# Products of constants in front of TensorE's waits in a two-layer trunk of attention and experts

## The chip, the cores and the metric

The kernel runs on one core of one Trainium2 chip. The metric is the device time of one execution in microseconds (us), less is better; the median of several executions is compared.

## What is computed

A trunk of two layers on 512 tokens (one sequence, d = 1024). Layer 0 mixes with FoX attention (16 heads of 64, a forget gate per head), layer 1 with multi-head latent attention (MLA). After each mixer stands a mixture of 16 experts with gated MLPs; each token goes to 2 of them. All is float32.

```python
for i in range(DEPTH):                                   # 2 layers
    mod = silu(c) @ w_ada[i] + b_ada[i]
    sh1, sc1, g1, sh2, sc2, g2 = split(mod, 6)
    h = rmsnorm(x, mix_norm[i]) * (1 + sc1) + sh1
    y = fox_mixer(h, ...) if i % 2 == 0 else mla_mixer(h, positions, ...)
    x = x + g1 * y
    h = rmsnorm(x, ffn_norm[i]) * (1 + sc2) + sh2
    x = x + g2 * hier_moe(h, ...)

def hier_moe(h, ...):        # group top-1 of 4, expert top-2 of the 4 in that group
    combine = sum(one_hot(expert_id, 16) * w, axis=1)    # (tokens, 16), two nonzero in a row
    a, u = einsum('td,edf->tef', t, w_gate), einsum('td,edf->tef', t, w_up)     # f = 256
    return einsum('tef,efd->td', silu(a) * u * combine[..., None], w_down)
```

## The kernel before, in words

The work runs in tiles of 128 tokens, with up to 512 columns in a PSUM bank. A float32 product is made of three fp32r products of split operands (`mm3`, L128 high x high, L129 high x low weights, L130 low x high). A framework with tile pools adds the semaphores and reorders independent instructions of an engine (MLA's attention apart, which is written in a fixed order); `self.after(i)` (L1265) asks that what follows be issued behind instruction i on its engine. PSUM has banks with tags: `mm`, `s`, `pt` have two buffers each, `pv` and `ad` one (function `ps`).

The places that matter here, in the order of the program:

- **FoX stack** (`fox_stack`, L519): the normalised q and k rows (`qn`, L506) are transposed by TensorE into `ps_pt`.
- **Output projection** (`out_products`, L937 in the functions below), two halves of 512 columns by four token tiles; `moe_token` and `moe_last` then normalise each token tile, transpose it and multiply it with the router (L1051, L1076, L1079).
- **Ranks** (`dispatch`): VectorE makes the 0/1 table A of token by expert (L1119); TensorE turns it into a rank of each token within its expert by products with triangular tables (L1134, L1141). Later VectorE makes `aux`, 4 columns for each token and expert: its number and its weight in three bf16 parts (the casts L1180).
- **Slots** (`place`, `slots`, `picked`): for an expert VectorE compares the ranks with 0..99 (L1204, `oh`), TensorE picks `aux` by `oh` (four products, L1216), VectorE writes the indices `gi` (L1208), GpSimd gathers the expert's up to 100 rows `xe` from DRAM (L1269). Experts 0 to 3 are placed first, with the column of token numbers alone (`place(e, 1)`); their weights come later by L1367 (16 products of 3 columns). Experts from 4 on are placed inside the loop over experts, with all four columns, so their picks need the finished `aux`.
- **Experts** (loop of `moe`): in step e the kernel calls `place(e + 4)`, then `expert_in` (TensorE transposes `xe` into `ps_pt`, L1281; ScalarE and VectorE write `xTh`, L1283, and `xTl`, L1284), in step 0 for experts 0 and 1; then `expert_up` (24 products of 512 columns into `ps_s`) and, of the expert before, `expert_down` (`ps_mm`, L128 to L130 and L1318). Weights are loaded by SyncE's queue and split into high and low part (`weh` L136 on ScalarE, `wel` L137 on VectorE or GpSimd).
- **Result** (`result_add`): the experts' rows come back by indirect DMA (`yd` in DRAM, layer 0 into `yg`, layer 1 into `xo`), and TensorE adds them up (L1422, and L1425 for the rows of the last experts, which were kept in SBUF).

Of the kernel before, what the change touches and what calls it, by code (L numbers as in the profile page):

```python
# [19 lines left out]
P = 128  # L20
# [27 lines left out]
NFIRST = 2  # L48
HPOOL = (3,)
# [31 lines left out]
class Trunk:  # L81
# [4 lines left out]
    def setup(self):  # L86
# [28 lines left out]

        self.first32 = c.tile([P, 1], F32, name="first32")
# [7 lines left out]

    def mm3(self, out, lhs, rhs, start, stop):
        mm = self.nc.tensor.matmul
        (lh, ll), (rh, rl) = lhs, rhs
        mm(out, lh, rh, start=start, stop=False)  # L128
        mm(out, lh, rl, start=False, stop=False)  # L129
        mm(out, ll, rh, start=False, stop=stop)  # L130
# [249 lines left out]
    def pv(self, pool, V2, PT, h, hl, oT):  # L380
# [59 lines left out]
    def fox_begin(self, hT, pool):  # L440
# [7 lines left out]
        def rows(t, ks):  # L448
            for k in ks:
                self.mm3(ps[t][:, :384], [x[:, k, t * P:(t + 1) * P] for x in hT], ws[k], k == 0, k == KC - 1)  # L450
# [39 lines left out]
    def fox_proj(self, ws, hT, t):  # L490
        ts = slice(t * P, t * P + P)
        p = self.ps("mm")
        for k in range(KC):
            self.mm3(p[:, :384], [x[:, k, ts] for x in hT], ws[k], k == 0, k == KC - 1)
        return p
# [16 lines left out]
    def fox_stack(self, qn, g2, KL, slots):  # L512
# [198 lines left out]
    def mla_latents(self, x, xs, kept, begun, lat, pool, slots, fills):  # L711
# [13 lines left out]
        for t in range(NT):  # L725
# [3 lines left out]
            self.result_add(xt, two[t], t, kept, "ss")  # L729
# [205 lines left out]
    def out_products(self, p, oS, ws, t, ks):  # L935
        for k in ks:
            self.mm3(p, [x[:, t * P:(t + 1) * P] for x in oS[k]], ws[k], k == 0, k == KC - 1)  # L937
# [17 lines left out]
    def proj_out(self, pool, oS, ws, ps, wsrc, g1, x_in, after, finish):  # L955
# [7 lines left out]
        for c in range(2):  # L963
# [78 lines left out]
    def moe_token(self, x, G, SH, wr, lg, t, pool):  # L1042
# [4 lines left out]
        q = self.ps("s")[:, 0:4 + N_EXP]  # L1047
# [12 lines left out]
    def moe_last(self, x, G, SH, wr, lg, pool):  # L1060
# [8 lines left out]
        for half in range(2):  # L1069
# [4 lines left out]
            p = self.ps(("pv", "ad")[half]).rearrange("p (k t) -> p k t", k=4)  # L1074
# [3 lines left out]
            for k in range(k4):  # L1078
                nc.tensor.matmul(q, xT[:, k, :], w[:, half * k4 + k, :], start=(half == 0 and k == 0),  # L1079
                                 stop=(half == 1 and k == k4 - 1))  # L1080
# [16 lines left out]
    def dispatch(self, lg, mp, pool, tmp, lay):  # L1097
# [26 lines left out]
        diff, rest = tok(self.ps("pt")), tok(self.ps("pt"))  # L1124
# [86 lines left out]
    def picked(self, oh, aux):  # L1211
# [3 lines left out]
        for t in range(NT):  # L1215
            self.nc.tensor.matmul(q[:CAP, 0:n], oh[:, t, :], aux[:, t, :], start=(t == 0), stop=(t == NT - 1))  # L1216
# [56 lines left out]
    def expert_in(self, xe, pool):  # L1273
# [14 lines left out]
    def expert_up(self, ws, xT, w, pool):  # L1288

        nc = self.nc  # L1290
        p = self.ps("s")[:CAP]
# [8 lines left out]
    def expert_down(self, a, ws, gi, g2, pool, keep=False, rows=None):  # L1300
# [13 lines left out]
        for c in range(2):  # L1314
# [3 lines left out]
            nc.tensor.matmul(p, hT[:, 1, :], ws[1][:, cs], start=False, stop=True)  # L1318
# [15 lines left out]
    def moe(self, lay, rk, g2, loads, raws, downs, xp, kept):  # L1334
# [21 lines left out]
        for e in range(PLACE):  # L1356
            with self.after(placed[-2] if e > 1 else None):
# [19 lines left out]
        for e in range(N_EXP + 1):  # L1377
            if e < N_EXP:
# [36 lines left out]
    def result_add(self, xt, two, t, kept, tags, done=None):  # L1415
# [14 lines left out]
    def combine(self, x, out, lay, kept, ring):  # L1430
# [6 lines left out]
        for t in range(NT):  # L1437
# [4 lines left out]
            self.result_add(xs[t], two[t], t, kept, [CTAG[(2 * t + c) % 3] for c in range(2)], done)  # L1442
# [200 lines left out]
```

## Time and profile before

| | |
|---|---|
| median of three executions | 1106.43 us (1104.5, 1106.43, 1106.9) |
| the profiled execution | 1113.87 us |
| its span (first to last instruction) | 1112.1 us |
| mean granted clock of TensorE | 0.929 of full speed |
| busy: TensorE, VectorE, ScalarE, GpSimd | 87%, 74%, 54%, 32% |

The profiled execution took 7.4 us more than the median; 1.8 us of it lie outside the span. A busy TensorE may still run at the half clock, so its busy time is read together with the granted clock.

### The profile page before, as it was taken

The numbers are of one execution on the slowest core, as the hardware profiler recorded it, in microseconds if no ns is written. First come the engines' busy times: TensorE is split into PE (matmuls) and PEld (weight loads), VectorE is DVE, ScalarE is ACT, GpSimd is POOL, SyncE is SP. The second block draws the span as 40 slices with busy tenths as digits, with TensorE's granted clock in tenths as the row PEclk, the third lists the DMA queues.
The fourth block names the chain that finished last, engine by engine and source line by source line (L and its number), as shares of the span: only waits on it lengthen the run. The fifth ranks groups of instructions, "written<-read, shape, count | busy, mean of one in ns | idle before, by whom it ended". The sixth has DMA issues, their size and how long they took to land.

```text
span 1112.1 us, 16807 instructions
## 1 busy us (share of the span) xinstructions
PE 970.9 (87%) x5298; PEld 737.9 (66%) x5298; DVE 819.1 (74%) x1918; ACT 600.0 (54%) x1318; POOL 351.0 (32%) x376
## 2 busy tenths in 40 slices
PE   4788989999799858999987989989897939999996
PEld 2476868877777746666645766878686826666663
DVE  4375757777953888998866569989863778998874
ACT  5244636566742426666644446879663417566640
POOL 0011101111312655434322006555422454543332
PEclk9788989999899859999998989999898959999998
DMA  7845547577555668999969858111215787999956
GB/s 265 246 133 183 164 143 221 170 244 241 183 198 157 244 207 279 313 315 342 373 184 340 319 171 298 49 58 48 86 58 174 263 264 220 313 320 325 372 222 228
DMA packets 135732, 248.34 MB, mean 223 GB/s; under 512 B 27677, under 2 KB 56735, under 8 KB 135639
## 3 DMA queue, kind: packets, MB, share of 16 engines
q1 hardware_dynamic: 123410, 211.74, 58.0%
q0 software_dynamic: 11648, 33.39, 9.6%
q10 hardware_dynamic: 580, 2.10, 0.5%
q8 instruction: 43, 0.70, 0.3%
q14 instruction: 51, 0.41, 0.1%
HBM read 222.63 MB, written 24.55 MB: 222 GB/s over the span
## 4 chain that ended last, share of the span: by engine, by line
PE 52%; DMA 19%; DVE 12%; issue 7%; SPq 4%; ACT 3%; POOL 3%; POOLq 0%; ACTq 0%; DVEq 0%
PE ps_mm L128 6%; PE ps_mm L129 6%; PE ps_mm L130 6%; PE ps_s L398 4%; DMA wraw<-in_w_ada_dram 4%; DMA xe<-hd,gi 4%; PE ps_s L129 3%; PE ps_ad L207 3%; PE ps_s L130 3%; PE ps_s L128 3%; DMA wraw<-in_moe_w_gate_dram 3%; PE ps_pv L387 3%; PE ps_pt L364 3%; PE ps_mm L1318 2%; DMA wa<-in_w_ada_dram 2%
## 5 line engine op out<-in xcount | busy, mean ns | idle before, releaser
L136 ACT CAST weh<-wraw 128x1024 fp32r<-128x1024 f32 x128 | 133.1, 1050 | 50.7 <-PE ps_s L130 44.4
L357 POOL TENSOR_SCALAR prob<-prob,smx 128x128 f32<-128x128 f32 (+3 forms) x128 | 70.4, 551 | 283.5 <-DVE smx L356 211.8
L137 DVE TENSOR_TENSOR wel<-wraw,weh 128x1024 fp32r<-128x1024 f32 x90 | 137.9, 1557 | 19.7 <-ACT weh L136 19.3
L129 PE MATMUL ps_s<-wel,xTh 128*100 128x512 f32 x256 | 108.5, 424 | 4.5 <-DVE wel L137 3.9
L128 PE MATMUL ps_s<-weh,xTh 128*100 128x512 f32 x256 | 106.9, 419 | 3.9 <-issue 3.4
L137 POOL TENSOR_TENSOR wel<-wraw,weh 128x1024 fp32r<-128x1024 f32 x38 | 94.6, 2492 | 49.5 <-ACT weh L136 39.3
L130 PE MATMUL ps_s<-weh,xTl 128*100 128x512 f32 x256 | 107.3, 419 | 0.0
L128 PE MATMUL ps_mm<-wqh,hTh 128*128 128x384 f32 x240 | 87.2, 365 | 2.5 <-ACT hTh L317 1.9
L129 PE MATMUL ps_mm<-wql,hTh 128*128 128x384 f32 x240 | 85.3, 357 | 0.0
L130 PE MATMUL ps_mm<-wqh,hTl 128*128 128x384 f32 x240 | 84.4, 354 | 0.0
L366 ACT CAST pth<-ps_pt 128x128 fp32r<-128x128 f32 (+3 forms) x128 | 53.2, 423 | 35.7 <-PE ps_pt L364 35.4
L364 PE MATMUL ps_pt<-ident,prob 128*128 128x128 f32 x320 | 57.6, 283 | 12.8 <-POOL prob L357 7.5
L1318 PE MATMUL ps_mm<-wraw,hT 128*100 128x512 f32 x128 | 65.3, 591 | 0.0
L367 DVE TENSOR_TENSOR ptl<-ps_pt,pth 128x128 fp32r<-128x128 f32 (+3 forms) x128 | 60.5, 480 | 5.5 <-ACT pth L366 5.0
L1269 POOL DMA_INDIRECT xe<-hd,gi x32 | 47.9, 1498 | 45.7 <-PE ps_pt L1281 16.2
L128 PEld LDWEIGHTS ps_s<-weh,xTh 128*100 128x100 f32 x256 | 44.0, 173 | 22.7 <-issue 7.9
L129 PEld LDWEIGHTS ps_s<-wel,xTh 128*100 128x100 f32 x256 | 43.9, 172 | 21.0 <-DVE wel L137 5.2
L207 PE MATMUL ps_ad<-wraw,crep 128*32 128x512 f32 x320 | 44.6, 638 | 13.8 <-DMA wraw<-in_w_ada_dram 13.8
L1328 POOL DMA_DIRECT2D yd<-ye x29 | 17.6, 606 | 123.6 <-DVE ye L1319 71.5
L130 PEld LDWEIGHTS ps_s<-weh,xTl 128*100 128x100 f32 x256 | 43.6, 170 | 17.6 <-issue 3.9
L352 DVE CUSTOM_DVE_ANT_0 prob<-ps_s,negc 128x128 f32<-128x128 f32 (+1 forms) x64 | 31.0, 487 | 32.8 <-PE ps_pt L364 20.8
L364 PEld LDWEIGHTS ps_pt<-ident,prob 128*128 128x128 f32 x320 | 40.2, 145 | 21.4 <-POOL prob L357 10.0
(480 smaller groups left out, 2802.4 us busy)
## 6 DMA issues: line engine op xcount, KB each, us to landing
wraw<-in_w_ada_dram SPq DMA_DIRECT2D x84, 512.0 KB
wraw<-in_moe_w_gate_dram SPq DMA_DIRECT2D x128, 256.0 KB
wraw<-in_moe_w_up_dram SPq DMA_DIRECT2D x128, 256.0 KB
wraw<-in_moe_w_down_dram SPq DMA_DIRECT2D x64, 512.0 KB
wraw<-in_fox_w_in_dram SPq DMA_DIRECT2D x64, 192.0 KB
yd<-ye POOLq DMA_DIRECT2D x29, 400.0 KB, 6.9
wa<-in_w_ada_dram SPq DMA_DIRECT2D x12, 512.0 KB
negc<-cumd SPq DMA_DIRECT2D x16, 256.0 KB
```

What stands on the lines that cost most here:

```text
L128: mm(out, lh, rh, start=start, stop=False)
L129: mm(out, lh, rl, start=False, stop=False)
L130: mm(out, ll, rh, start=False, stop=stop)
L136: self.nc.scalar.copy(hi, src)
L137: (eng or self.nc.vector).tensor_sub(lo, src, hi.bitcast(F32))
L207: mm = nc.tensor.matmul(p[32 * g:32 * g + 32, :], self.crep[:, k, :], ws[g // 2][:, (g % 2) * 512:(g % 2) * 512 + 512], start=(k == 0), st ...
L357: nc.gpsimd.tensor_scalar(pr[:, :n], pr[:, :n], st[:, 2:3], 1.0, op0=OP.mult, op1=OP.mult)
L364: nc.tensor.transpose(p[:, j, :], pr[:, j * P:(j + 1) * P], self.ident)
L366: nc.scalar.copy(PT[0][sl], p[:, :i + 1, :])
L367: nc.vector.tensor_sub(PT[1][sl], p[:, :i + 1, :], PT[0][sl].bitcast(F32))
L1269: return self.nc.gpsimd.indirect_dma_start(out=xe, out_offset=None, in_=self.hd, in_offset=bass.IndirectOffsetOnAxis(ap=gi, axis=0), bound ...
L1318: nc.tensor.matmul(p, hT[:, 1, :], ws[1][:, cs], start=False, stop=True)
```

## The change

A helper `busy(p, n, behind)` issues n bf16 products of the constant identity with itself (128 columns, repeated four times: 512) into a PSUM tile p, whose contents the next products or transposes overwrite; nobody reads these products. They are issued behind a given instruction. A table `BUSY` gives the number for each place (a pair: layer 0 and layer 1). In all 146 products are added, each with its load of weights; no instruction of the other engines is added or removed. Some calls return their last product so that `busy` can stand behind it.

```diff
+BUSY = {"stack": 14, "out": 6, "norm": 5, "last": 3, "rank": (10, 18), "slot": (5, 9), "xe0": (4, 0), "up0": (8, 0),
+        "xe1": (0, 14), "result": (20, 16)}
...
+    def busy(self, p, n, behind=None):
+
+        with self.after(behind):
+            for _ in range(n):
+                self.nc.tensor.matmul(p.rearrange("p (k t) -> p k t", k=4), self.identb,
+                                      self.identb.unsqueeze(1).to_broadcast([P, 4, P]), start=True, stop=True)
...
             p = self.ps("pt")
+            if u == 0 and not self.stacked:
+                self.busy(p, BUSY["stack"], self.qkv)
+                self.stacked = True
...
+                if ps and t == 0:
+                    self.busy(self.ps("pt"), BUSY["out"], self.out_last if c else self.pv_last)
...
+        if t == NT - 2:
+            self.busy(q, BUSY["norm"], self.out_last)
...
+            if half == 0:
+                self.busy(p, BUSY["last"], self.out_last)
...
+        diff, rest = self.ps("pt"), self.ps("pt")
+        self.busy(diff, BUSY["rank"][lay], self.routed)
...
-            self.nc.tensor.matmul(q[:CAP, 0:n], oh[:, t, :], aux[:, t, :], start=(t == 0), stop=(t == NT - 1))
+            self.pick = self.nc.tensor.matmul(q[:CAP, 0:n], oh[:, t, :], aux[:, t, :], start=(t == 0), stop=(t == NT - 1))
...
+            if half == 0 and busy:
+                self.busy(p, busy, behind)
...
+        p = self.ps("s")
+        if busy:
+            self.busy(p, busy, self.turned)
...
+            if e == PLACE - 1:
+                self.busy(self.ps("mm"), BUSY["slot"][lay], self.pick)
...
-                        xT[a] = self.expert_in(xes[a], ep)
+                        xT[a] = self.expert_in(xes[a], ep, (BUSY["xe0"], BUSY["xe1"])[a][lay] if e == 0 else 0,
+                                               self.pick if a == 0 else self.turned)
...
-                mid[e] = self.expert_up(ws[e], xT[e], w[e], ep)
+                mid[e] = self.expert_up(ws[e], xT[e], w[e], ep, BUSY["up0"][lay] if e == 0 else 0)
...
+            if t == 0 and c == 0:
+                self.busy(p, BUSY["result"][lay], self.down_last if lay else None)
```

Line numbers of the changed kernel are higher: L128 to L130 become L139 to L141, L1216 becomes L1240, L1281 L1308, L1367 L1399; the added products are L133.

TensorE's order in layer 0, from the picks to expert 0's first products, before (L1216 x1 the last pick of expert 3, L1281 x8 the transposes of expert 0's rows, x4 half of expert 1's):

```order
L1216 LDWEIGHTS oh
L1216 MATMUL ps_pv<-aux,oh 100x1
L1281 MATMUL ps_pt<-ident,xe 128x100 x8
L128 MATMUL ps_s<-weh,xTh 100x512
L129 MATMUL ps_s<-wel,xTh 100x512
L1281 MATMUL ps_pt<-ident,xe 128x100 x4
L130 MATMUL ps_s<-weh,xTl 100x512
```

And with the change (L1399 stands 16 times; L1240 x4 columns are the picks of experts 4, 5 and 6 in turn; L133 into `ps_pt` is "xe0", into `ps_s` is "up0"; the pair of a pick and four transposes, shown once, stands twice):

```order
L1240 MATMUL ps_pv<-aux,oh 100x1
...
L1399 MATMUL ps_pv<-aux,oh 100x3
...
L1240 MATMUL ps_pv<-aux,oh 100x4
L133 LDWEIGHTS identb
L133 MATMUL ps_pt<-identb 128x512
...
L1308 MATMUL ps_pt<-ident,xe 128x100 x8
...
L1240 MATMUL ps_pv<-aux,oh 100x4
L1308 MATMUL ps_pt<-ident,xe 128x100 x4
...
L133 MATMUL ps_s<-identb 128x512
...
L139 MATMUL ps_s<-weh,xTh 100x512
```

In the call of `place(4)` just ahead, `self.pick` became the last pick of expert 4, and "xe0" is issued behind that one. So the weights' picks, the picks of experts 4 to 6 and all transposes of expert 1 now stand in front of expert 0's first product; before, the 16 picks of the weights stood behind its first 23 products and expert 4's picks later still.

In layer 1 "xe0" and "up0" are zero. There the order of before was, row for row, that of layer 0 shown first. With the change it is (L133 into `ps_pt` is "xe1", 14 times):

```order
L1240 MATMUL ps_pv<-aux,oh 100x1
L1308 MATMUL ps_pt<-ident,xe 128x100 x8
L139 MATMUL ps_s<-weh,xTh 100x512
L140 MATMUL ps_s<-wel,xTh 100x512
L133 LDWEIGHTS identb
L133 MATMUL ps_pt<-identb 128x512
...
L1308 MATMUL ps_pt<-ident,xe 128x100 x4
L141 MATMUL ps_s<-weh,xTl 100x512
```

Here only the 14 products came in, between expert 0's second product and expert 1's transposes; the picks stayed where they were.

## Rows read from the trace of the kernel before

**Rows 1.** The page of the profile, its head, the busy time of TensorE and VectorE (first row of part 1), and TensorE's granted clock in 40 equal slices of 27.8 us.

```profile
span 1112.1 us, 16807 instructions
...
PE 970.9 (87%) x5298; PEld 737.9 (66%) x5298; DVE 819.1 (74%) x1918; ACT 600.0 (54%) x1318; POOL 351.0 (32%) x376
...
PEclk9788989999899859999998989999898959999998
```

**Rows 2.** What TensorE waited for (view of waits): consumer and its line, releaser, total us, times, longest us.

```profile
PE ps_ad L207 <- DMA wraw<-in_w_ada_dram: 13.8, 5, 4.7
...
PE ps_pt L1134 <- DVE A L1119: 11.9, 2, 7.3
...
PE ps_s L1422 <- DMA yg<-yd,pos: 7.8, 1, 7.8
...
PE ps_pv L1216 <- DVE gi L1208: 6.3, 6, 3.5
...
PE ps_s L1422 <- DMA xo<-yd,pos: 5.8, 1, 5.8
PE ps_pt L519 <- DVE qn L506: 4.9, 1, 4.9
...
PE ps_mm L128 <- DVE yo L974: 3.0, 2, 1.9
```

**Rows 3.** Stretches of the span: us of the stretch; busy us and instructions of PE, PEld, DVE, ACT, POOL; granted clock of PE; DMA share; GB/s.

```profile
65.50:70.50 5.00, 0.10 (x2) 0.08 (x2) 4.83 (x15) 3.76 (x11) 0.00 (x0) 1.00 0.39 115
70.50:77.40 6.90, 6.33 (x20) 5.96 (x21) 5.28 (x22) 1.85 (x9) 0.00 (x0) 0.51 0.37 118
408.60:411.90 3.30, 3.29 (x10) 2.33 (x11) 3.10 (x17) 0.85 (x2) 0.71 (x1) 0.51 0.87 216
440.00:450.00 10.00, 10.00 (x42) 6.64 (x41) 6.09 (x9) 4.66 (x6) 2.85 (x3) 0.87 1.05 300
581.40:589.20 7.80, 0.04 (x1) 0.04 (x1) 1.38 (x3) 3.86 (x9) 2.03 (x2) 0.79 0.83 279
589.20:592.80 3.60, 3.60 (x7) 1.85 (x7) 2.83 (x6) 0.00 (x0) 1.04 (x1) 0.51 1.03 415
916.50:920.50 4.00, 3.97 (x12) 2.99 (x13) 1.42 (x5) 1.54 (x2) 0.00 (x0) 0.51 0.89 238
1084.50:1090.40 5.90, 0.07 (x1) 0.08 (x1) 3.20 (x6) 1.22 (x2) 4.48 (x5) 0.77 0.81 256
1090.40:1094.60 4.20, 4.20 (x8) 2.36 (x8) 1.41 (x3) 0.00 (x0) 3.37 (x3) 0.51 0.95 352
```

**Rows 4.** TensorE in order of time, the transposes behind the first FoX projection (start us, us, line, operation, in brackets the idle time before and what ended it).

```profile
70.45 0.61 PE L519 MATMUL ps_pt<-ident,qn 128*128 128x128 f32 x2 [4.90 <-DVE qn L506]
```

**Rows 5.** TensorE in order of time, layer 0, from the fourth expert's pick to expert 0's products.

```profile
401.11 0.42 PE L1216 MATMUL ps_pv<-aux,oh 128*100 128x1 bf16 x4 [1.76 <-DVE gi L1208]
403.68 1.58 PE L1281 MATMUL ps_pt<-ident,xe 100*128 100x100 f32 x8 [2.15 <-DMA xe<-hd,gi]
408.61 0.75 PE L128 MATMUL ps_s<-weh,xTh 128*100 128x512 f32 x1 [3.35 <-issue]
...
409.58 0.87 PE L1281 MATMUL ps_pt<-ident,xe 100*128 100x100 f32 x4
...
411.92 0.39 PE L128 MATMUL ps_s<-weh,xTh 128*100 128x512 f32 x1
412.15 0.39 PE L129 MATMUL ps_s<-wel,xTh 128*100 128x512 f32 x1
...
416.30 0.87 PE L1367 MATMUL ps_pv<-aux,oh 128*100 128x3 bf16 x16
...
421.23 0.31 PE L1216 MATMUL ps_pv<-aux,oh 128*100 128x4 bf16 x4
422.51 0.47 PE L129 MATMUL ps_s<-wel,xTh 128*100 128x512 f32 x1 [0.98 <-DVE wel L137]
```

**Rows 6.** VectorE in order of time in the same stretch: two compares of ranks, one instruction of the overflow count, and the first of the casts that write aux (the last one ends at 412.39).

```profile
399.94 1.05 DVE L1204 TENSOR_TENSOR oh<-slot,rk 128x400 bf16<-128x400 bf16 x2
...
401.33 5.35 DVE L1187 TENSOR_SCALAR nt<-ce 128x16 f32<-128x16 f32 x1
...
410.73 0.23 DVE L1180 CAST aux<-we 128x64 bf16<-128x64 f32 x1
```

**Rows 7.** GpSimd in order of time in the same stretch.

```profile
401.99 4.65 POOL L137 TENSOR_TENSOR wel<-wraw,weh 128x1024 fp32r<-128x1024 f32 x2
```

**Rows 8.** TensorE in order of time, layer 0, at the end of expert 1's up products.

```profile
438.14 1.25 PE L1281 MATMUL ps_pt<-ident,xe 100*128 100x100 f32 x8 [1.33 <-DMA xe<-hd,gi]
```

**Rows 9.** TensorE in order of time, layer 1, expert 0's first products and the transposes of expert 1's tokens.

```profile
910.16 0.63 PE L129 MATMUL ps_s<-wel,xTh 128*100 128x512 f32 x1
916.53 0.92 PE L1281 MATMUL ps_pt<-ident,xe 100*128 100x100 f32 x4 [5.74 <-DMA xe<-hd,gi]
...
917.67 0.63 PE L128 MATMUL ps_s<-weh,xTh 128*100 128x512 f32 x1
918.10 0.63 PE L129 MATMUL ps_s<-wel,xTh 128*100 128x512 f32 x1
```

**Rows 10.** TensorE in order of time, layer 1, the last expert product and the first product of the result.

```profile
1083.47 1.02 PE L1318 MATMUL ps_mm<-wraw,hT 128*100 128x512 f32 x2
1090.33 2.07 PE L1422 MATMUL ps_s<-xo,ident 128*128 128x512 f32 x2 [5.83 <-DMA xo<-yd,pos]
```

More of the change, by code (lines that the diff above doesn't have):

```diff
@@ L114, in setup @@
                        allow_small_or_imprecise_dtypes=True)
+        self.stacked = False
         self.first32 = c.tile([P, 1], F32, name="first32")
@@ L129, in mm3 @@
         mm(out, lh, rl, start=False, stop=False)
-        mm(out, ll, rh, start=False, stop=stop)
+        return mm(out, ll, rh, start=False, stop=stop)
     def split(self, shape, src, name, eng=None, pool=None):
@@ L449, in rows @@
             for k in ks:
-                self.mm3(ps[t][:, :384], [x[:, k, t * P:(t + 1) * P] for x in hT], ws[k], k == 0, k == KC - 1)
+                self.qkv = self.mm3(ps[t][:, :384], [x[:, k, t * P:(t + 1) * P] for x in hT], ws[k], k == 0, k == KC - 1)
         def gates(ks):
@@ L493, in fox_proj @@
         for k in range(KC):
-            self.mm3(p[:, :384], [x[:, k, ts] for x in hT], ws[k], k == 0, k == KC - 1)
+            self.qkv = self.mm3(p[:, :384], [x[:, k, ts] for x in hT], ws[k], k == 0, k == KC - 1)
         return p
@@ L728, in mla_latents @@
                 self.advance(fills)
-            self.result_add(xt, two[t], t, kept, "ss")
+            self.result_add(0, xt, two[t], t, kept, "ss")
             nc.scalar.dma_start(x[t * P:(t + 1) * P, :], xt)
@@ L936, in out_products @@
         for k in ks:
-            self.mm3(p, [x[:, t * P:(t + 1) * P] for x in oS[k]], ws[k], k == 0, k == KC - 1)
+            self.out_last = self.mm3(p, [x[:, t * P:(t + 1) * P] for x in oS[k]], ws[k], k == 0, k == KC - 1)
     def out_begin(self, oT, wsrc, slots, out):
@@ L1073, in moe_last @@
                 pool.tile([P, k4, P], F32, name="xTl", tag="hj")
-            p = self.ps(("pv", "ad")[half]).rearrange("p (k t) -> p k t", k=4)
+            p = self.ps(("pv", "ad")[half])
+            if half == 0:
+                self.busy(p, BUSY["last"], self.out_last)
+            p = p.rearrange("p (k t) -> p k t", k=4)
             for k in range(k4):
@@ L1078, in moe_last @@
             for k in range(k4):
-                nc.tensor.matmul(q, xT[:, k, :], w[:, half * k4 + k, :], start=(half == 0 and k == 0),
-                                 stop=(half == 1 and k == k4 - 1))
+                self.routed = nc.tensor.matmul(q, xT[:, k, :], w[:, half * k4 + k, :], start=(half == 0 and k == 0),
+                                               stop=(half == 1 and k == k4 - 1))
             nc.scalar.activation(self.ps("pv" if half else "ad"), x[:, cs], AF.Square, accum_out=ssq[:, half:half + 1])
@@ L1271, in gather, with expert_in @@
             bounds_check=S - 1, oob_is_err=True)
-    def expert_in(self, xe, pool):
+    def expert_in(self, xe, pool, busy=0, behind=None):
         nc = self.nc
@@ L1286, in expert_in, with expert_up @@
         return xT
-    def expert_up(self, ws, xT, w, pool):
+    def expert_up(self, ws, xT, w, pool, busy=0):
         nc = self.nc
-        p = self.ps("s")[:CAP]
+        p = self.ps("s")
+        if busy:
+            self.busy(p, busy, self.turned)
+        p = p[:CAP]
         for k in range(KC):
@@ L1413, in collect, with result_add @@
         return out
-    def result_add(self, xt, two, t, kept, tags, done=None):
+    def result_add(self, lay, xt, two, t, kept, tags, done=None):
         nc = self.nc
@@ L1440, in done @@
                 self.nc.sync.dma_start(out[t * P:(t + 1) * P, cs], xs[t][:, cs])
-            self.result_add(xs[t], two[t], t, kept, [CTAG[(2 * t + c) % 3] for c in range(2)], done)
+            self.result_add(lay, xs[t], two[t], t, kept, [CTAG[(2 * t + c) % 3] for c in range(2)], done)
     def overflow(self, layer, rk1, end, base, novf, g2, xp, mp, raw, sp):
```

14 lines of the change are left out of this document (8 added, 6 removed).

## The prediction

> **What bounds the kernel now.** I read the page first: TensorE is busy 970.9 of 1112.1 us, and the row of its granted clock has slices at 8 tenths and below [rows 1]. So two things can be had on TensorE: its waits, and the time after a wait in which it runs at the half level. The view of waits says which waits are long [rows 2]: 11.9 us for the table A in two waits (the longer 7.3, so the shorter 4.6), 7.8 and 5.8 for the gathered results, 4.9 for `qn`, 3.5 for `gi`. The stretches behind them were read last [rows 3]: in 70.5 to 77.4, 408.6 to 411.9, 589.2 to 592.8, 916.5 to 920.5 and 1090.4 to 1094.6 the granted clock is 0.51, and TensorE is busy nearly throughout. [...] The added products are to keep it up; they shorten no wait. What they can give back is about half of the busy time in those stretches, and what they can cost is delay of what stands behind them on TensorE.
>
> **The price of a product.** A bf16 product of 512 columns is not in the trace. The nearest rows are fp32r products of 512 columns: from 411.92 to 412.15, 0.23 us at the full clock [rows 5], and from 917.67 to 918.10, 0.43 us at half [rows 9]. I take these; below them is no reason to go, since the columns are the same. [...]
>
> **Stack, 14.** 14 x 0.23 = 3.2 us stand in the wait of 4.90 ahead of L519 [rows 4] and end before `qn` comes; 1.7 us of the wait are left. In the stretch behind, 6.33 us of work run at 0.51 [rows 3], worth up to 3.1 us. Does a wait of 1.7 us keep the clock? Rows speak both ways: after the wait of 0.98 us at 422.51 the products run at full pace [rows 5], after that of 1.33 us at 438.14 the clock of 440 to 450 is 0.87 [rows 3, 8]. I take somewhat under half: -1.2, ends 0 and -3.1.
>
> **Result, 20 and 16.** In layer 0, 20 x 0.23 = 4.6 us of the wait of 7.8 [rows 2] are filled, 3.2 us stay empty; the 3.60 us behind it [rows 3] hold at most 1.8. With so much left I take -0.3. In layer 1, TensorE ends L1318 at 1084.5 and starts L1422 at 1090.33 after 5.83 us [rows 10]; 16 x 0.23 = 3.7 are filled, 2.1 stay. Behind it 4.20 us run at 0.51 [rows 3], worth 2.1, and nothing but the result and its store comes after, so whatever is saved counts in full. Half: -1.1, ends 0 and -2.1.
>
> **xe1, 14, layer 1.** They run between expert 0's second product and the transposes at 916.53, which wait 5.74 us for the gather [rows 9]. The clock there is already 0.51, so 14 x 0.43 = 6.0 us, 0.3 more than the wait, unless the clock rises within them. Behind, 3.97 us at 0.51 [rows 3] give 2.0 back. Net -1.6; at the other end 0, if the next split weights or the next gather set the pace there.
>
> **Rank and slot.** Layer 0: 10 x 0.43 = 4.3 in a wait of 4.6. Layer 1: 18 products, 4.1 to 7.7 us in a wait of 7.3; slot 9, 2.1 to 3.9 us in a wait of 3.5 [rows 2]. They can overrun by 0.4 each if the clock stays low, and speed up the small products behind if it rises: together -0.2, ends -0.8 and +0.8. Slot 5 in layer 0 delays a pick whose expert (3) is needed much later; nothing.
>
> **Out, norm, last.** In layer 1, six products at half clock are 2.6 us where the wait for `yo` is 1.9 [rows 2], so they overrun by 0.7; but the projection is a chain through VectorE's `yo` and the x tiles, not TensorE alone. Norm and last put 8 products, 1.8 us, in front of the last two router tiles of each layer, where VectorE's normalisation comes later still and hides most. Together +0.4, ends 0 and +2.5.
>
> **xe0 and up0, layer 0: the term that decides.** Not the 12 products but the place counts. "xe0" is issued behind expert 4's pick, and expert 4's pick needs `aux`. So expert 0's transposes, at 403.68 before [rows 5], wait for the end of the routing on VectorE. That end was 412.39: a stall of 5.35 us at 401.33 [rows 6], lying with GpSimd's split of weights (4.65 us at 401.99 [rows 7]), then the routing, with the first cast of `aux` at 410.73. Without the three subtractions of `xTl` that lay between the casts (they need the transposes, so now come later) `aux` is ready near 411.
>
> From there, in a row on TensorE: three compares of about 0.53 (1.05 for two [rows 6]) with the 16 picks of the weights beside them, to 412.6; expert 4's pick 0.42, to 413.0; "xe0" 4 x 0.43 = 1.7, to 414.7; eight transposes 1.58, to 416.3; twice a pick and four transposes, 2 x (0.42 + 0.87) = 2.6, to 418.9; "up0", 8 x 0.23 = 1.8, to 420.7, if the clock is up by then (8 x 0.43 = 3.4 otherwise, 422.3). Expert 0's first product starts near 420.6 instead of 408.61: **12.0 us late**.
>
> What comes back by 450: TensorE's waits of 0.98 and 1.33 us [rows 5, 8] and some 0.6 of smaller ones, 2.9, because the split weights and gathered rows are then long there; the six products that ran at half clock from 408.6 to 411.9, 6 x 0.20 = 1.2; the half clock near 440 (0.87 of 10 us means 2.6 us at half, 1.3 back, with the tail before 440 taken as 1.8); and the work that now lies ahead, 0.87 (L1367), 0.31 (pick of expert 4), eight transposes and two picks, about 2.3 in pitch. Together 8.2. From 440 on TensorE is busy 10.00 of 10 us [rows 3], with experts following one another without a wait, so what is not back by then is kept: 12.0 - 8.2 = **+3.8**, ends +1.5 (aux earlier by what VectorE is spared, full clock in up0) and +8.5 (only the moved work and the 1.2 come back).
>
> **Reordering elsewhere.** The framework orders some of VectorE's, ScalarE's and SyncE's instructions differently in the FoX stretch. No row has a price for that; the waits for `w_ada` there, 13.8 us with one of 4.7 [rows 2], show what a load that moves can matter. Zero, ends -2.5 and +2.5.
>
> **Sum.** -1.2 - 0.3 - 1.1 - 1.6 - 0.2 + 0.4 + 3.8 = -0.2 us. The profiled execution of 1113.87 us (span 1112.1, 1.8 outside it) is 7.4 above the median 1106.43; the sum is a difference and is put on the median: 1106.2 us. A measurement of this kernel tells about 0.2%, 2.2 us, from no change.
>
> **Rivals.**
>
> *The clock holds through the shortened waits.* The remains of 1.7 and 2.1 us would be like the 0.98 us at 422.51, not like 438.14. Then the whole price comes back: 3.1 + 2.1 + 2.0 + 1.8 = 9.0 instead of 4.2, so -0.2 - 4.8 = -5.0, about 1101.4. For it: in 65.5 to 70.5 the clock is still 1.00 over a wait of 4.9 us and in 581.4 to 589.2 it is 0.79 in the mean [rows 3], so it doesn't fall at once. [...] Against: 438.14.
>
> *The layer-0 delay is absorbed.* If the loads of weights bound the experts (DMA share 1.05 in 440 to 450 [rows 3]) and not TensorE, a late start would cost little: 0 instead of +3.8 gives -4.0, 1102.4. Against it, TensorE has no wait in that stretch.
>
> *The layer-0 delay is not made up (slower).* VectorE runs the picks' reads, compares and `xTl` before the split weights; if these then come late, the waits near 422 and 438 stay and the half clock with them. It takes only the splits to be as late as the start. +8.5 instead of +3.8: +4.5, 1110.9. It decides once more than 2.4 us beyond my sum are lost there.
>
> *The products do nothing for the clock (slower).* The clock falls in each remaining wait, as after 438.14, and only the delay is left: +3.8 + 0.4 = +4.2, 1110.6.
>
> **Chances.** My sum 0.40, the clock holds 0.17, absorbed 0.15, not made up 0.18, nothing for the clock 0.10. My sum is likely within 0.2%, with 0.03 of it on each side. Faster 0.35, same 0.34, slower 0.31. The range goes from 1100 (both faster rivals partly) to 1111.5 (the slower ones and a little of the reordering); my own case alone is 1104 to 1108.5.
>
> **What would show it.** In layer 0, expert 0's first product near 12 us later against the fourth pick, TensorE without waits from there to 450, and expert 1's end 2 to 6 us later than before against the start of the dispatch. In layer 1, products behind 916 at pitch 0.23, not 0.43. At the end, granted clock of the first 4 us of the result: 0.5 or 1.0. Behind the FoX wait the same. I am wrong if the picks of experts 4 to 6 don't hold up expert 0, if the FoX stretch moves by more than 2.5 us, or if a product costs clearly more than 0.23 at full clock.

## The result and the profile after

The changed kernel took 1095.97 us in the median of six executions, beside 1106.47 of the kernel before: ratio 0.9888, interval 0.986 to 0.9915. Forecast was 1106.2 with a range from 1100. So the change gained 10.5 us by the medians and about 12 by the ratio, where the sum said none.

The page after (span, busy time of TensorE, its granted clock in 40 slices), to be read against [rows 1]:

```profile
span 1092.4 us, 17112 instructions
...
PE 989.2 (91%) x5444; PEld 738.3 (68%) x5444; DVE 816.8 (75%) x1918; ACT 598.8 (55%) x1318; POOL 349.3 (32%) x376
...
PEclk9699999999998969999998989999899989999999
```

The mean granted clock is 0.956 instead of 0.929. The profiled span is 19.7 us shorter, though the medians differ by 10.5: the profiled execution of before lay 7.4 us above its median, that of after 1.8 below. Differences between these two traces alone therefore say too much, and the experiments carry traces of 16 more executions.

What TensorE waited for after (view of waits: consumer, releaser, total us, times, longest), against [rows 2]:

```profile
PE ps_pv L1399 <- DVE aux L1204: 9.2, 1, 9.2
PE ps_ad L218 <- DMA wraw<-in_w_ada_dram: 8.4, 4, 4.3
...
PE ps_s L1457 <- DMA yg<-yd,pos: 5.4, 2, 3.8
...
PE ps_pt L1158 <- DVE A L1141: 3.3, 1, 3.3
...
PE ps_s L1457 <- DMA xo<-yd,pos: 2.1, 1, 2.1
...
PE ps_pt L533 <- DVE qn L517: 1.8, 1, 1.8
...
PE ps_pv L1240 <- DVE gi L1232: 1.0, 4, 0.2
```

The waits for A and `gi` (11.9 and 6.3 before) are mostly filled. The waits for `qn` (4.9 before) and the two results (7.8 and 5.8 before) are shorter by what the products fill. One long wait is new, 9.2 us for `aux` on L1399. And the waits for `w_ada`, which no product was put in front of, fell from 13.8 to 8.4 us.

Stretches of after, columns as in [rows 3]:

```profile
65.50:70.50 5.00, 3.58 (x18) 1.51 (x16) 4.81 (x15) 3.44 (x10) 0.00 (x0) 1.00 0.46 123
70.50:77.40 6.90, 5.71 (x25) 5.51 (x26) 5.77 (x23) 2.33 (x11) 0.00 (x0) 0.75 0.34 107
440.00:450.00 10.00, 10.00 (x48) 6.82 (x47) 9.62 (x12) 6.57 (x10) 4.69 (x4) 1.00 1.04 341
```

Behind `qn` the clock is 0.75 where it was 0.51; at 440 to 450 it is 1.00 where it was 0.87.

Layer 0's dispatch on TensorE after, in order of time, against [rows 5]:

```profile
385.31 0.42 PE L1240 MATMUL ps_pv<-aux,oh 128*100 128x1 bf16 x4 [0.25 <-DVE gi L1232]
...
397.32 1.47 PE L1399 MATMUL ps_pv<-aux,oh 128*100 128x3 bf16 x16 [9.16 <-DVE aux L1204]
399.46 0.42 PE L1240 MATMUL ps_pv<-aux,oh 128*100 128x4 bf16 x4 [0.68 <-DVE sw L1402]
...
401.41 1.49 PE L1308 MATMUL ps_pt<-ident,xe 100*128 100x100 f32 x8
...
405.17 1.89 PE L133 MATMUL ps_s<-identb 128*128 128x512 bf16 x8
406.71 0.58 PE L139 MATMUL ps_s<-weh,xTh 128*100 128x512 f32 x1
```

This is what the prediction described: the 16 picks of the weights wait for `aux`, then expert 4's pick, then "xe0", the transposes, "up0", and expert 0's first product at 406.71.

The table below sets the stages of all executions that were traced side by side. Each number is the time between two landmarks in TensorE's order of time: *FoX* from the first to the last mask product; *dispatch and experts 0* from the first pick to the first product of layer 0's result; *result 0* from there to MLA's first high x high score; *MLA* to the last one; *experts 1* from layer 1's first down product (`ps_mm<-wdh,hsh`) to the last; *end* from there to the last kept-row product of the result. Two stretches are not in the table: from the last mask product to the first pick (70.0 to 72.3 us in all) and from MLA's last score to layer 1's first down product (99.2 to 106.5).

| kernel | FoX | dispatch and experts 0 | result 0 | MLA | experts 1 | end |
|---|---|---|---|---|---|---|
| before | 241.6 | 191.6 | 98.2 | 145.9 | 147.4 | 24.2 |
| before again (e1) | 242.6 | 189.9 | 96.9 | 143.3 | 147.2 | 24.3 |
| stack 5 (e2) | 241.7 | 191.7 | 94.8 | 144.2 | 147.9 | 24.6 |
| stack 6 (e3) | 228.5 | 190.6 | 97.2 | 143.5 | 149.6 | 24.4 |
| stack 14 (e4) | 226.8 | 189.5 | 96.9 | 145.6 | 147.7 | 24.2 |
| all but stack (e5) | 240.7 | 194.6 | 100.3 | 148.4 | 141.4 | 22.1 |
| change without xe0, up0 (e6) | 229.6 | 190.7 | 100.8 | 148.6 | 141.4 | 22.0 |
| layer 1 only (e7) | 239.5 | 190.1 | 95.7 | 142.9 | 141.4 | 23.7 |
| negc in two buffers (e8) | 237.0 | 192.3 | 96.1 | 143.6 | 147.9 | 24.6 |
| stack and layer 1 (e9) | 227.0 | 192.3 | 96.9 | 144.9 | 141.4 | 24.1 |
| xe1 only (e10) | 239.9 | 191.8 | 97.4 | 143.9 | 141.4 | 24.0 |
| layer 1 without xe1 (e11) | 242.8 | 189.1 | 97.2 | 144.0 | 149.8 | 22.0 |
| change again (e12) | 227.2 | 194.4 | 101.7 | 143.4 | 141.4 | 22.9 |
| w_ada first, no products (e13) | 229.6 | 191.2 | 97.8 | 147.4 | 145.0 | 23.8 |
| e9 with xe0, up0 (e14) | 226.8 | 196.1 | 97.6 | 147.9 | 141.4 | 22.3 |
| e9 with result 20 (e15) | 229.8 | 190.0 | 102.4 | 148.9 | 141.4 | 24.0 |
| e9 with out, norm, last (e16) | 226.8 | 192.4 | 96.1 | 149.1 | 141.4 | 22.1 |
| the change | 226.6 | 193.0 | 101.8 | 143.0 | 141.4 | 23.5 |

A column changes level where a part comes in, whatever the others do: FoX at stack 6 (and in e13, with the order alone), experts 1 at xe1, dispatch at xe0 and up0 (by little: 193.0 and above with them, 192.4 and below without), result 0 at result 20.

### The profile page after: what moved, and what is told of

It reads as the page before. It is cut to its first block, busy times and chain, and to the rows that moved or that the text cites. A ratio compares the mean times of both kernels' runs of the same rounds, so it can differ in the third digit from the quotient of the medians.

```text
span 1092.4 us, 17112 instructions
## 1 busy us (share of the span) xinstructions
PE 989.2 (91%) x5444; PEld 738.3 (68%) x5444; DVE 816.8 (75%) x1918; ACT 598.8 (55%) x1318; POOL 349.3 (32%) x376
## 4 chain that ended last, share of the span: by engine, by line
PE 62%; DMA 17%; DVE 11%; issue 5%; SPq 2%; ACT 2%; POOL 2%; POOLq 0%; DVEq 0%; ACTq 0%
PE ps_mm L139 7%; PE ps_mm L141 7%; PE ps_mm L140 7%; PE ps_s L140 5%; PE ps_s L139 5%; PE ps_s L141 5%; DMA yd<-ye 4%; PE ps_s L409 4%; DMA wraw<-in_w_ada_dram 4%; PE ps_pv L398 3%; PE ps_mm L1348 3%; PE ps_ad L218 3%; PE ps_pt L375 3%; PE ps_pt L1308 2%; DMA wa<-in_w_ada_dram 2%
## 5 line engine op out<-in xcount | busy, mean ns | idle before, releaser
L148 DVE TENSOR_TENSOR wel<-wraw,weh 128x1024 fp32r<-128x1024 f32 x90 | 142.0, 1603 | 12.4 <-ACT weh L147 11.6
L141 PE MATMUL ps_s<-weh,xTl 128*100 128x512 f32 x256 | 107.1, 418 | 0.0
L139 PE MATMUL ps_s<-weh,xTh 128*100 128x512 f32 x256 | 104.9, 411 | 0.1
L139 PE MATMUL ps_mm<-wqh,hTh 128*128 128x384 f32 x240 | 86.0, 360 | 2.8 <-ACT hTh L328 1.8
L141 PE MATMUL ps_mm<-wqh,hTl 128*128 128x384 f32 x240 | 83.4, 350 | 0.0
L139 PEld LDWEIGHTS ps_s<-weh,xTh 128*100 128x100 f32 x256 | 43.2, 169 | 19.2 <-issue 4.8
L1358 POOL DMA_DIRECT2D yd<-ye x29 | 17.5, 605 | 119.0 <-DVE ye L1349 97.8
L141 PEld LDWEIGHTS ps_s<-weh,xTl 128*100 128x100 f32 x256 | 42.6, 166 | 18.9 <-issue 5.3
L1281 ACT CAST wdh<-wraw 128x1024 fp32r<-128x1024 f32 x32 | 33.3, 1047 | 39.9 <-PE ps_mm L141 36.2
L139 PEld LDWEIGHTS ps_mm<-wqh,hTh 128*128 128x128 f32 x240 | 47.0, 197 | 6.3 <-ACT hTh L328 2.1
```

The source lines that it names most:

```text
L141: return mm(out, ll, rh, start=False, stop=stop)
L148: (eng or self.nc.vector).tensor_sub(lo, src, hi.bitcast(F32))
```

## The experiments

Two theories stand against each other. *Kept clock*: the products gain by the clock they keep up behind the waits, each place for itself, as the sum had it. *Order*: the products enter the framework's own estimate of when each engine is free, so it puts other instructions in another order, far from the products, and that order gains or loses.

### The stack alone, and the order without products

First the kernel before a second time, no edit.

> The kernel before, unchanged, profiled a second time, so that two profiles of one program can be laid side by side. If the profile of before was a slow specimen (it lay 7.4 us above the median), this one shows a time near 1106 us and the end of FoX's attention (last mask product, 326.4 us before) several us earlier. If FoX's end and the stretch of the layer-1 experts repeat within 1 us, what the changed kernel gained there comes from its code.

It took 1110.4 us in its one execution. FoX, the layer-1 experts and the end repeat within 1 us (242.6, 147.2, 24.3), so what the change gained there is no accident of one trace. MLA moved by 2.6.

Then the stack's products alone, every other entry of the table zero. The edit of e2; e3 has 6 in place of 5, e4 has 14:

```diff
-BUSY = {"stack": 14, "out": 6, "norm": 5, "last": 3, "rank": (10, 18), "slot": (5, 9), "xe0": (4, 0), "up0": (8, 0),
-        "xe1": (0, 14), "result": (20, 16)}
+BUSY = {"stack": 5, "out": 0, "norm": 0, "last": 0, "rank": (0, 0), "slot": (0, 0), "xe0": (0, 0), "up0": (0, 0),
+        "xe1": (0, 0), "result": (0, 0)}
```

> Only the stack products, and 5 of them instead of 14; no other place. The order of all other instructions is then that of before on every engine. Theory of the order (FoX gained because its instructions stand otherwise): no change, ratio 0.999 to 1.001. Theory of the clock (the products in the wait keep the clock up): 5 x 0.23 = 1.2 us leave 3.7 us of the wait empty, so also little, 0 to -0.5 us.

> Only the stack products, 6 of them: one more than in the run beside it, but with 6 the framework orders FoX's instructions on all engines as in the changed kernel. Theory of the order: most of the gain of FoX comes with the sixth product, 5 us or more, ratio 0.995 or below. Theory of the clock: as with 5, 0 to -0.5 us.

> Only the stack products, all 14, with FoX in the order of the changed kernel. Theory of the order: the same as with 6, within 1.5 us. Theory of the clock: 1 to 3 us faster than with 6, and the granted clock behind the wait for qn above 0.7 where before it was 0.51.

With 5: ratio 1.0009 (0.9989 to 1.003). With 6: 0.9904 (0.987 to 0.9938). With 14: 0.9884 (0.986 to 0.9908). **One product more, 0.22 us of work, gained about 12 us.** Eight more gained 2 by the medians, which is within the intervals. In the traces they raise the clock of 70.5 to 77.4 from 0.52 to 0.75, and from the last product of the first projection to the first mask product it takes 19.6 us instead of 20.6; the FoX column begins behind that stretch. The fourteen stack products alone give as much as the whole change.

What differs between 5 and 6 is seen on SyncE's queue (start, us, queue, loads). With 5:

```profile
74.50 10.61 SPq L185 DMA_DIRECT2D wraw<-in_w_ada_dram  x3
87.85 0.33 SPq L569 DMA_DIRECT2D negc<-cumd  x1
95.81 3.92 SPq L185 DMA_DIRECT2D wraw<-in_w_ada_dram  x3
```

With 6:

```profile
74.75 11.59 SPq L185 DMA_DIRECT2D wraw<-in_w_ada_dram  x5
91.52 0.33 SPq L569 DMA_DIRECT2D negc<-cumd  x1
92.83 4.41 SPq L185 DMA_DIRECT2D wraw<-in_w_ada_dram  x3
```

And on TensorE (`ps_ad` is where the products of `w_ada` accumulate; the lower row is FoX's last mask product). With 5:

```profile
105.21 1.93 PE L217 MATMUL ps_ad<-wraw,crep 128*32 128x512 f32 x8 [2.55 <-DMA wraw<-in_w_ada_dram]
...
326.29 0.23 PE L409 MATMUL ps_s<-maskneg,identb 128*128 128x128 bf16 x1
```

With 6:

```profile
78.68 1.06 PE L217 MATMUL ps_ad<-wraw,crep 128*32 128x512 f32 x8
...
314.33 0.23 PE L409 MATMUL ps_s<-maskneg,identb 128*128 128x128 bf16 x1
```

The stretch 84.5 to 120 (columns as in [rows 3]), with 5 and then with 6:

```profile
84.50:120.00 35.50, 32.30 (x187) 25.74 (x186) 20.84 (x72) 16.78 (x47) 4.29 (x8) 0.90 0.58 179
```

```profile
84.50:120.00 35.50, 35.02 (x227) 28.47 (x226) 24.91 (x85) 19.34 (x56) 5.68 (x10) 1.00 0.66 208
```

With 6 the first products of `w_ada` in FoX run at 78.68, before the second projection; with 5 they came at 83.21, behind it. They free their buffers sooner, so five loads of `w_ada` and not three go ahead of the load of `negc`, which stands in the queue until the head before has been read. With 5 the load of `w_ada` behind `negc` then stands longer still (what SyncE's queue waited for from 60 to 120 us, and VectorE):

```profile
SPq L185 <- DVE rstq L159: 7.7, 1, 7.7
...
SPq L569 <- DVE smx L366: 2.9, 1, 2.9
```

```profile
94.82 0.96 DVE L147 TENSOR_TENSOR wql<-wraw,wqh 128x768 fp32r<-128x768 f32 x1 [0.75 <-ACT wqh L146]
```

`negc` holds the queue for 2.9 us. The load behind it waits another 7.7 and goes out at 95.81, as VectorE ends its split of the FoX weights (`wql`, 95.78), which reads a buffer of `wraw`; the profile names `rstq`, the instruction beside it, which reads none. With 5 the fourth group of products then waits 2.55 us for its weights at 105.21, and its eight products take 1.93 us, 1.8 times the 1.06 of the eight at 83.21 (granted clock 0.90 in the mean over the stretch); with 6 it doesn't wait, and the clock is 1.00. The row of before, 13.8 us of waits for `w_ada` [rows 2], was the sign of it; 8.3 of them stand in FoX.

That is not the whole of the 13 us. From the first mask product to the last, TensorE is idle for 20.2 us with 5 and 11.8 with 6, and busy 4.8 us less, at a mean clock of 0.99 instead of 0.95; the waits for `w_ada` fall from 9.1 to 4.8 us. The gain stands in two places: 9.9 us up to the 17th mask product, where the loads act, and 6.2 behind the 53rd; between them 2.9 are lost. In the last part TensorE waits once for GpSimd with 5, and with 6 no wait is over 1 us:

```profile
303.88 1.08 PE L374 MATMUL ps_pt<-ident,prob 128*128 128x128 f32 x4 [5.06 <-POOL prob L367]
```

To take the products out of the argument, e13 makes that order without them: in the kernel before, the products of the first three blocks of `w_ada` in FoX get priority.

```diff
+EARLY = {(0, 1, k) for k in range(3)}
...
                     if head:
                         together.enter_context(self.after(head))
+                    if head or (i, pair, k) in EARLY:
                         together.enter_context(self.tc.high_priority())
```

> The kernel before with no added product; only the products of the first three blocks of w_ada in FoX (accumulated into ps_ad) are given priority, so that the first of them stand ahead of the second FoX projection, as they do in the changed kernel, and SyncE's queue then has nearly the order of the changed kernel in FoX. Theory of the order: FoX's last mask product near 314 us instead of 326, ratio 0.992 or below. If the added products are needed for the gain: no change, 0.999 to 1.001.

Ratio 0.9917 (0.9888 to 0.9946), on TensorE:

```profile
77.67 1.07 PE L209 MATMUL ps_ad<-wraw,crep 128*32 128x512 f32 x8
...
314.57 0.23 PE L401 MATMUL ps_s<-maskneg,identb 128*128 128x128 bf16 x1
```

FoX takes 229.6 us without one added product, with the gain in the same two places (9.1 and 5.9 us against e2). The order carries the gain; what in it spares the late wait for `prob` was not tested. That the queue's block at `negc` is the cause within it was tried by giving `negc` a second buffer:

```diff
-                negc = pool.tile([P, 512], F32, name="negc", tag="negc", bufs=1)
+                negc = pool.tile([P, 512], F32, name="negc", tag="negc", bufs=2)
```

> The kernel before with two buffers instead of one for negc, the row of forget sums that each FoX head loads on SyncE's queue; no added products. TensorE's order in the first two thirds of FoX is that of before. The load of the second head then doesn't hold the queue until the first head has read its own, and three loads of w_ada behind it start earlier. If the place of negc among the loads of w_ada is why the order of the changed kernel is faster, the first heads gain: the ninth score (119.3 us) comes 2 us or more earlier and the whole is 3 us or more faster, ratio 0.997 or below. If TensorE's own order is the cause: no change.

Ratio 0.9955 (0.9935 to 0.9974), but not for the reason given: the ninth score came at 118.47, 0.9 earlier, not 2; the third load of `negc` then waits 2.9 us at the same point (88.30), and the load of `w_ada` behind it 7.3 for VectorE, which the second buffer doesn't touch. FoX's gain of about 5 us comes behind the thirty-third score (218.98, as in before; the forty-first is 2.7 earlier), where the framework's order differs too. So `negc` alone is not it; what is shown is the earlier place of `w_ada`'s products with all that follows from it.

### Layer 1

The layer-1 places alone, all together (e7); e10 keeps only its xe1, e11 all but xe1.

```diff
-BUSY = {"stack": 14, "out": 6, "norm": 5, "last": 3, "rank": (10, 18), "slot": (5, 9), "xe0": (4, 0), "up0": (8, 0),
-        "xe1": (0, 14), "result": (20, 16)}
+BUSY = {"stack": 0, "out": 0, "norm": 0, "last": 0, "rank": (0, 18), "slot": (0, 9), "xe0": (0, 0), "up0": (0, 0),
+        "xe1": (0, 14), "result": (0, 16)}
```

> Only the layer-1 places rank 18, slot 9, xe1 14 and result 16; the rest as in before. By the terms of the prediction -0.2 - 1.6 - 1.1 = -2.9 us, ratio 0.997. The two profiles of the kernels with and without them speak for more, 8 us or so between the end of the projection and the end: then 0.993 or below.

> Only xe1, 14 products, in layer 1. With it the framework orders the layer-1 experts as in the changed kernel. Theory of the order: most of the 11.7 us of the layer-1 places are here, ratio 0.994 or below, and the time from expert 0's down product to the last one falls from 147.4 us by about 6. Theory of the kept clock, by the prediction's term: -1.6 us, 0.9985.

> Rank 18, slot 9 and result 16 in layer 1, without xe1. The order of the layer-1 experts stays near that of before. Theory of the order: -1 to -4 us, ratio 0.996 to 0.999, by the kept clock alone, and the experts' stretch at 147 us. If the kept clock is what counts: 0.993 or below.

Ratios 0.9894 (0.9856 to 0.9933), 0.9923 (0.9895 to 0.9951) and 0.9992 (0.9969 to 1.0014). xe1 is the part that counts, and where it counts is not behind its own products: experts 1 takes 141.4 us in every kernel with xe1 14, to the tenth, and 145.0 to 149.8 without (149.8 in e11, where 147 was expected). The kernel before (e1) and xe1 alone (e10), TensorE at the first picks of four columns in the loop and at the transposes of expert 4's rows:

```profile
926.53 0.30 PE L1216 MATMUL ps_pv<-aux,oh 128*100 128x4 bf16 x4 [0.57 <-DVE sw L1370]
...
943.30 0.33 PE L1281 MATMUL ps_pt<-ident,xe 100*128 100x100 f32 x1 [2.22 <-DMA xe<-hd,gi]
```

```profile
919.85 0.31 PE L1239 MATMUL ps_pv<-aux,oh 128*100 128x4 bf16 x4
...
937.77 1.16 PE L1307 MATMUL ps_pt<-ident,xe 100*128 100x100 f32 x8
```

GpSimd's gathers (`xe<-hd,gi`) at the same place, e1 and then e10:

```profile
932.09 3.48 POOL L1269 DMA_INDIRECT xe<-hd,gi  x1 [7.09 <-PE ps_pt L1281]
```

```profile
925.09 1.86 POOL L1292 DMA_INDIRECT xe<-hd,gi  x1 [0.19 <-issue]
928.47 2.33 POOL L1292 DMA_INDIRECT xe<-hd,gi  x1 [1.52 <-PE ps_pt L1307]
```

And VectorE's index for that gather, e1 and then e10:

```profile
931.64 0.15 DVE L1208 TENSOR_SCALAR gi<-ps_pv 100x1 int32<-100x1 f32 x1
```

```profile
920.91 0.15 DVE L1231 TENSOR_SCALAR gi<-ps_pv 100x1 int32<-100x1 f32 x1
```

In e1 the pick of expert 4 stands at 926.53, VectorE writes the index at 931.64, the gather goes out at 932.09, and TensorE waits 2.22 us for the rows at 943.30, with about half the pace behind (products of 512 columns every 0.43 us from 944.46 to 947.45, in e10 every 0.23 from 939.00; granted clock 0.92 in the mean of 928 to 950, in e10 1.00). (The profile names TensorE's transposes as the gather's releaser; the index came within 0.3 us of their end.) In e10 the framework puts the picks 7 us further ahead, at 919.85; the index is written at 920.91, the gathers go out from 925.09, and the transposes at 937.77 don't wait. All traces agree: that index is written 0.15 us before layer 1's first down product in the eight without xe1, and 6.2 to 7.8 before it in the ten with it. From that product to the last, TensorE waits 3.6 us in e1 (2.2 here, 1.4 for split weights) and not at all in e10. So the cause is read from rows that all agree; this order was not made without the products, as e13 makes it in FoX. Earlier picks are what layer 0 paid for; here, where the pick's inputs are long there, they pay.

### Layer 0, the projection, and what is left

The changed kernel with "stack" at 0 is e5. The changed kernel without the two places of layer 0's first experts is e6:

```diff
-        "xe0": (4, 0), "up0": (8, 0),
+        "xe0": (0, 0), "up0": (0, 0),
```

> Every place of the change except the stack, so FoX stands in the order of before. By the terms of the prediction without the stack (-0.3 - 1.1 - 1.6 - 0.2 + 0.4 + 3.8 = +1.0) ratio 1.000 to 1.002. If the products themselves and the kept clock bring the gain, 0.993 or below.

> The changed kernel without the products of xe0 and up0 in layer 0, so expert 0's transposes no longer stand behind expert 4's pick; all else is as in the change. If the late start of layer 0's experts costs what the prediction put on it (+3.8, ends 1.5 and 8.5), this is 2 to 6 us faster than the changed kernel, ratio 0.983 to 0.987 to before, with expert 0's first product some 12 us earlier. If the delay is absorbed: the same as the changed kernel, 0.989.

e5: 1.0037 (1.0014 to 1.0061). Without the stack the change makes the kernel slower, although its layer-1 places alone gain 11 us. That this lies near the expected 1.000 to 1.002 is luck: a gain that the sum did not have meets losses that it did not have. e6: 0.9886 (0.9851 to 0.992), as the changed kernel, which misses the expectation of 2 to 6 us. Expert 0's first product does come 12 us earlier (394.30, not 406.71), and the dispatch column gives back 2.3 to 3.7; but FoX takes 2.4 to 3.0 us more there, and MLA 148.6 where the changed kernel has 143, which eats it.

A kernel of the two parts that gain (e9), beside the changed kernel itself (e12, no edit):

```diff
+BUSY = {"stack": 14, "out": 0, "norm": 0, "last": 0, "rank": (0, 18), "slot": (0, 9), "xe0": (0, 0), "up0": (0, 0),
+        "xe1": (0, 14), "result": (0, 16)}
```

> Stack 14 and the layer-1 places rank 18, slot 9, xe1 14, result 16; nothing in layer 0's dispatch and result, nothing in the projection and the router. The two parts alone gave ratios 0.9884 and 0.9894 and touch different stretches: if they add up, 0.978 (24 us). If part of the gain of each is given back to a load that both had hurried, 0.983 or above.

> The changed kernel once more, beside the others of this call. Ratio 0.986 to 0.991, and slower than stack and layer 1 alone by what the places of layer 0, the projection and the router cost: about 10 us if the parts add up.

e9: 0.9821 (0.979 to 0.9852), median 1089.67 us; the change on the same chip 0.9889 (0.9857 to 0.9922). **e9 beats both kernels**, the changed one by some 7 us; the two parts nearly add up. Then each of three remaining parts was added to e9: in e14 the first line, in e15 the second, in e16 the third.

```diff
+        "xe0": (4, 0), "up0": (8, 0)
+        "result": (20, 16)
+        "out": 6, "norm": 5, "last": 3
```

> Stack and layer 1 (ratio 0.982 alone), and the products of xe0 and up0 in layer 0 with them. The prediction's term: +3.8 us, so ratio 0.985 to 0.986, expert 0's first product 12 us later against the first pick, and the time from the first pick to the result of layer 0 3 to 5 us longer (189.1 without). If the delay is absorbed: 0.982 and 189 to 190.5.

> Stack and layer 1, and the 20 products in front of layer 0's result. The prediction's term: -0.3 us. The traces of kernels with and without them speak for a loss: about 4 us from the first product of the result to the first score of MLA (96.9 without), because the second token tile's rows are waited for earlier in TensorE's order; ratio then 0.985 to 0.986.

> Stack and layer 1, and the products of out, norm and last in the projection and the router. The prediction's term: +0.4 us, ends 0 and 2.5. So 0.982 to 0.984, and the time from MLA's last score to expert 0's down product of layer 1 within 2 us of 103.4.

Ratios 0.9892 (0.9854 to 0.9931), 0.9904 (0.9871 to 0.9937) and 0.9874 (0.9832 to 0.9916), on another chip, each to before on the same chip: 6 to 9 us above e9's ratio, and above all three expectations. The interval of e16 overlaps that of e9. Nor do the three add up: they make 23 us, and e12, which has them all, lies 7 above e9. The stages show a part of it. xe0 and up0: dispatch and experts 0 takes 196.1, 194.6, 194.4 and 193.0 us in the four kernels that have them, 190.9 in the mean of the others, **+3.6**. Result 20: result 0 takes 100.3 to 102.4, without it 94.8 to 98.2, in the means **+4.6**. In all three MLA costs 3 to 4 us more than in e9, though no product was added in it and TensorE's order there is the same in all kernels. But in e14 and e15 the stretch behind it, to layer 1's first down product, is 4.2 and 3.0 us shorter (99.2 and 100.4, in e9 103.4), and e14's traced span as a whole is 0.5 us shorter than e9's. So the traces show what xe0, up0 and result 20 cost in their own stages, and not the whole distance to e9. In e16 that stretch takes 106.5, outside its expectation; the other four kernels with out, norm and last have 100.3 to 102.3 there, so what these cost is open.

Why the 20 products lose, e9 and then the changed kernel (e12), TensorE at layer 0's result:

```profile
575.53 2.07 PE L1456 MATMUL ps_s<-yg,ident 128*128 128x512 f32 x2 [7.33 <-DMA yg<-yd,pos]
...
585.75 1.13 PE L1456 MATMUL ps_s<-yg,ident 128*128 128x512 f32 x2 [0.23 <-DMA yg<-yd,pos]
```

```profile
571.00 4.48 PE L133 MATMUL ps_s<-identb 128*128 128x512 bf16 x20 [0.90 <-PEq L1484]
577.44 1.12 PE L1457 MATMUL ps_s<-yg,ident 128*128 128x512 f32 x2 [1.96 <-DMA yg<-yd,pos]
...
588.13 2.04 PE L1457 MATMUL ps_s<-yg,ident 128*128 128x512 f32 x2 [3.95 <-DMA yg<-yd,pos]
```

The products run in the wait, and the first token tile starts with only 1.96 us left to wait. But the framework now also puts the second gather's products (`yg`, tiles 2 and 3) ahead of nearly all of MLA's first projection: 3.95 us of wait at 588.13, where e9 had other work and 0.23. That this order is the cause was not tested by itself.

## Why the prediction was wrong, point by point

**Where it failed.** The step "Reordering elsewhere": *"Zero, ends -2.5 and +2.5."* It was -13 (FoX 242.0 us in the mean of before, e1 and e2; 228.5 to 229.6 in e3 and e13), and so its own sign of being wrong came, a FoX stretch that moves by more than 2.5 us. The prediction had one right row in hand, the waits for `w_ada`, and took the new order as noise about zero. It put the whole 13.8 us into FoX, where 8.3 stand, and took them as a thing that a moved load might only shift. It counted neither the lower clock behind the waits of FoX (0.95 in the mean in e2 and 0.99 in e3; 4.8 us of busy time between them) nor the wait of 5.1 us for `prob`.

**xe1**, -1.6 (its own 0.3 and 2.0 make -1.7) with ends 0 and -2.0: the measured -6.0 (147.4 to 141.4) lies outside. The term priced the stretch behind the products; the gain was the gather of a later expert.

**Result 20**, -0.3: measured +4.6, of the other sign. The wait was sized rightly, the new place of the second tile's products was not looked for.

**xe0 and up0**, +3.8 (ends 1.5 and 8.5): measured +3.6. From the first pick to expert 0's first product it is 22.8 us in the changed kernel and 11.1 before, 11.7 late (up to 13.2 in the other three) where 12.0 was worked out, and TensorE then runs from 406.7 to beyond 450 without a wait. The mechanism and its place held. That the size came out so well is in part luck. Counted from the first pick, the four kernels are 6.7 us behind the others at the first down product, 4.6 at experts 6 to 9, 0.2 at expert 11 and 3.7 at the last. What was late at 450 was not simply kept, and why it swings later was not looked into.

**Stack by the clock**, -1.2: -1.0 in its own stretch (20.6 to 19.6 us, e3 to e4), and -1.7 and -2.0 in e15 and e6, whose clock from 70.5 to 77.4 is 1.00. **Out, norm, last**, +0.4: open, see above. **Rank and slot**, -0.2: 0.9992 with result 16, within the interval.

**Result 16**, -1.1 with ends 0 and -2.1, because the rest of the wait might or might not hold the clock. Both happen. The changed kernel, and e14, each with its stretch behind the wait (columns as in [rows 3]):

```profile
1065.29 3.62 PE L133 MATMUL ps_s<-identb 128*128 128x512 bf16 x16
1071.01 1.41 PE L1457 MATMUL ps_s<-xo,ident 128*128 128x512 f32 x2 [2.11 <-DMA xo<-yd,pos]
```

```profile
1071.00:1075.00 4.00, 3.99 (x8) 2.15 (x8) 1.76 (x3) 0.00 (x0) 3.09 (x4) 0.59 0.93 326
```

```profile
1071.07 1.13 PE L1456 MATMUL ps_s<-xo,ident 128*128 128x512 f32 x2 [2.20 <-DMA xo<-yd,pos]
```

```profile
1071.00:1075.00 4.00, 3.89 (x13) 2.25 (x13) 1.51 (x3) 0.00 (x0) 3.06 (x3) 1.00 0.98 301
```

After the same 16 products and waits of 2.11 and 2.20 us, one runs at 0.59 and one at 1.00; the end takes 23.5 and 22.3 us. In the ten traces with these products (waits 2.1 to 2.6 us) the first 4 us behind the wait run at 1.00 in six, with an end of 22.0 to 22.9 us, and at 0.59 to 0.68 in four, with an end of 23.5 to 24.1; without the products the end takes 23.8 to 24.6. What decides between the two was not shown.

**The rivals.** "The clock holds" was the right side and the wrong reason: the whole price of the clock was 9.0 us, and e13 makes 9 of the 12 us without a product that could hold it. "Absorbed" is refuted by the dispatch column of the four kernels with xe0 and up0, and so is "nothing for the clock" by the clock rows (0.75 for 0.51 behind `qn`, 1.00 in six of ten behind the last wait). "Not made up" didn't happen.

**What stays open.** MLA's 143 to 146 us in twelve traces and 147 to 149 in six. No order of ScalarE's instructions there occurs on both levels, but each of the six has an order of its own, two traces of the kernel before differ by 2.6 themselves, and nothing was run to test it. The stages of the changed kernel add up to 16.5 us less than before (two traces of each), of which the medians show 10.5 to 12; its executions lie between 1090 and 1101.

## What to carry to other kernels

Where a framework orders instructions by its own estimate of time, an added instruction is a change of order everywhere behind it: compare the orders on every engine, find the stretches that differ, and look in each for a wait on a queue that the new order feeds earlier or later, before pricing the instruction itself. Test the cause by making the order without the instruction. And add such places one at a time: here the stack and xe1 brought the gain, and the places in layer 0's dispatch and result and in the projection together gave about a third of it back.

## What the runs showed of the hardware

A bf16 product of 512 columns cost 0.22 to 0.23 us at granted clock 1.00 (in the changed kernel 16 in 3.62 us at 1065.29; in e12 20 in 4.48 us at 571.00), as the fp32r rows had suggested (0.23, [rows 5]). The wait of 2.1 to 2.6 us behind the 16 products was followed by a granted clock of 1.00 over the first 4 us in six traces and of 0.59 to 0.68 in four. In the changed kernel, one of the four, the first two products behind the wait took 1.41 us and the clock was 0.50 from 1072.2 to 1075; in e9 and e15, two others, the first two took 1.12 us, as in e12 and e16 of the six, and the fall came behind them. Executions of one kernel spread over 9 us and more (before 1103.88 to 1112.95 in 17, the change 1089.95 to 1099.65 in six). The stages of a trace tell smaller parts apart than the medians do, but a stage such as MLA moved by 2.6 us between two traces of one kernel.
